# Weights stored in the order of their tiles and a weight stream of seven buffers, in a decoder block on one core

## The chip, the cores and the metric

The kernel runs on one core of one Trainium2 chip. The metric is device time in microseconds; each version is timed in several runs and one further execution is profiled.

## What is computed

One layer of a hybrid decoder block on 256 tokens of width 2048, in float32. Cut to what matters:

```
ada = silu(c) @ w_ada + b_ada                      # c: one row of 2048; w_ada: 2048 x 12288
sh1, sc1, gt1, sh2, sc2, gt2 = split(ada, 6)
u = rmsnorm(x, g_mix) * (1 + sc1) + sh1            # 256 x 2048
q, kc, vc, ks, vs, kw, vw, g_nsa, u_ssm, g_merge = split(u @ w_in)     # w_in: 2048 x 11312
kc, vc = compress(kc, w_ck1, w_ck2), compress(vc, w_cv1, w_cv2)        # w_c*1: 32 x 128 x 128
y_a = attention(q; compressed, selected, window keys and values; g_nsa)
y_s = gelu(s5_ssm(u_ssm))                          # complex diagonal recurrence, 128 groups x 64 states
y_b = y_s * sigmoid(y_s @ w_glu + b_glu)
h = x + gt1 * ((sig(gA) * y_a + sig(gB) * y_b) @ w_out)
h = h + gt2 * (relu(rmsnorm(h) * (1 + sc2) + sh2 @ w_up)^2 @ w_down)
return rmsnorm(h, g_final)
```

## The kernel before, in words

All weights go once through SBUF as a stream of **units**: one unit is a tile `raw` of 128 partitions x 1024 float32 (512 KB) with what is done to it (class `Unit`, line 199; `load` is lines 206 to 209, issued on SyncE's queue). Units of a product ("gemm" units) are split in two float32r parts: ScalarE copies `raw` to `hi` (line 116, helper `copy`), VectorE makes `lo = raw - hi` (line 119, helper `tt`), and TensorE multiplies three times, hi x hi, hi x lo, lo x hi (lines 310, 312, 313; for values lines 893 to 895). Other units are read by TensorE straight from `raw`: the first third of the conditioning (`ada1_units`, products at line 339), most of the other two thirds (`ada2_pe_units`, line 998) and the compression weights (`compress_units`, line 1101, two units at a time). A few conditioning units are accumulated on VectorE (`ada2_units`, line 128).

The order of the units is a list written out by hand at the end of `block_kernel`: conditioning woven with the first pass of the projection (S5 channels, kc/vc, the keys ks and kw, chunk by chunk of the 2048 rows), then values vs and vw woven with compression, the gate unit, the projections gA, q, gB (each woven with conditioning units), w_glu with the attention running beside it, w_out, w_up, w_down. There are 697 units; `run_units` (line 225) walks through them in this order and emits, at unit i, first the loads that are due, then hi, then the product of the unit two places back (`SPLIT`), then lo, then steps of the background generators: the S5 parameters, its scan and outputs, loads and stores of intermediate tensors, the attention. All engines take their instructions in the order in which they are emitted. Which background step stands at which unit is set by counts of units, not by time.

Three things set when a load starts. The pool `raw` has `RAW = 4` buffers, so the load of unit i + 3 is emitted at unit i and waits on SyncE until the last reader of the unit that held the buffer is done: VectorE's lo, or TensorE's product. SyncE works in order, so every later transfer on its queue waits behind that load: S5 parameters (lines 512 to 522), stores of S5 matrices (`s5_keep`, line 756), their reloads (`s5_matrices`, line 833), the attention's tensors (`attn_setup`, lines 1032 to 1045). And the transfers of SyncE and ScalarE share eight completion counters, used in turn, so a transfer also waits for the one eight places before it.

The source of a load decides the length of its rows in HBM. `four_k` reads four blocks of 128 x 256 columns of `w_ada` (rows of 1 KB), `ada2_pe_units` eight blocks of 128 x 128 (512 B), `compress_units` eight 128 x 128 matrices (512 B), the gate unit 16 x 48 columns (192 B); keys and values take two transfers of 128 x 512 (2 KB rows) each. All other weights come in rows of 4 KB, or 2 KB for `w_glu`.

The outputs of the S5 part (`s5_outputs`, line 836) run beside the gB projection, units 269 to 296: 16 steps, each of which turns a slice of the states for the next step (`turn`, two ScalarE copies into a tile `xs` of 4 KB per partition, two buffers), multiplies on TensorE (lines 858, 863, 868), adds on VectorE (line 128) and ends in a gelu on ScalarE (line 873).

Of the kernel before, what the change touches and what calls it, by code (L numbers as in the profile page):

```python
# [9 lines left out]
FT = mybir.dt.float32  # L10
# [15 lines left out]

RAW, HI, LO = 4, 3, 3
SPLIT = 2
# [52 lines left out]
@with_exitstack  # L81
def block_kernel(ctx, tc, cst_in, x, c, w_ada, b_ada, g_mix, w_in, w_ck1, w_ck2, pe_ck,
                 w_cv1, w_cv2, pe_cv, a_re, a_im, log_dt, b_re, b_im, c_re, c_im, d_skip,
                 w_glu, b_glu, w_out, g_mlp, w_up, w_down, g_final, out):
    nc = tc.nc
# [139 lines left out]
    def run_units(bgs):  # L225
        n = len(units)
        for b in bgs:
            b["done"] = 0
        ready = []
        loaded = count = 0  # L230
# [6 lines left out]
        for i, u in enumerate(units):  # L237
            now[0] = u.index = i
            while loaded < min(n, i + RAW):
                units[loaded].load()  # L240
                loaded += 1
            u.prep()
            if u.lo_first:
                u.prep_lo()
            if u.gemm:
                ready.append(u)
                while len(ready) > SPLIT or any(r.joint for r in ready[:-1]):
                    run_next()
            else:
                u.do(u)  # L250
            if not (u.lo_first):
                u.prep_lo()
            while i in later:
                for fn in later.pop(i):
                    fn()
            count += u.gemm
            for b in bgs:
                if b["start"] <= i:
                    if b.get("tick"):
                        span, at = b["end"] - b["start"] + 1, i - b["start"] + 1  # L260
                    else:
                        b.setdefault("from", count - 1)
                        span, at = max(1, gemms[min(b["end"], n - 1)] - b["from"]), count - b["from"]
                    want = min(b["total"], -(-b["total"] * at // span))
                    while b["done"] < want:
                        b["done"] += 1
                        next(b["gen"], None)
                    if i >= b["end"]:
                        for _ in b["gen"]:
                            pass  # L270
# [8 lines left out]
    def gemm_pass(src, col0, kts, ncol, k_first, k_last, xs, banks, finish, xprep=None, halves=None,  # L279
# [6 lines left out]
        def src_of(kt0):  # L286
            if halves is None:
                if per == 1:
                    return [(lambda r: r, src[kt0 * 128:(kt0 + 1) * 128, col0:col0 + ncol])]
                v = src[kt0 * 128:(kt0 + per) * 128, col0:col0 + ncol].rearrange("(k p) n -> p k n", p=128)  # L290
                return [(lambda r: r.rearrange("p (k n) -> p k n", k=per), v)]
            return [((lambda r, j=j: r[:, 512 * j:512 * j + 512]),
                     src[kt0 * 128:(kt0 + 1) * 128, h:h + 512]) for j, h in enumerate(halves)]

# [34 lines left out]

    def four_k(off, t0, n=256):  # L330

        return [(lambda r: r.rearrange("p (k n) -> p k n", k=4),
                 w_ada[0, t0 * 128:(t0 + 4) * 128, off:off + n].rearrange("(k p) n -> p k n", p=128))]

# [53 lines left out]
    def first_pass_units(ci):  # L388
        k0, k1 = chunks[ci]
        res = []  # L390
        for g in PASS:
            def finish(b, ps, g=g):
# [5 lines left out]
                else:  # L398
                    st = stage()
                    tt(st, ps, acc, OP.add)  # L400
                    A.dma_start(out=d_k[:, 2 * b:2 * b + 2, :], in_=st.rearrange("p (k t) -> p k t", k=2))
            kw = dict(halves=(C_KS, C_KW)) if g == 3 else {}
            col0 = (C_SSM, C_SSM + 1024, C_KC, 0)[g]
# [433 lines left out]
    def s5_outputs():  # L837
# [4 lines left out]
        def turn(ct):  # L842

            t = sp.tile([128, 1024], FT, tag="xs", name="xs", bufs=2).rearrange("p (r q c) -> p r q c", r=2, q=4)
            for r_ in range(2):
# [35 lines left out]
    def vs_units():  # L881
        made = {}

        def run(u, kt):
# [3 lines left out]
            for t in range(2):  # L888
                xh, xl = uh[:, kt, t * 128:t * 128 + 128], ul[:, kt, t * 128:t * 128 + 128]
                for s in range(2):  # L890
# [5 lines left out]
                    if kt == 15:  # L896
                        st = stage()
                        copy(st, o)
                        A.dma_start(out=d_v[:, t, s, :], in_=st)
        return [Unit([((lambda r, j=j: r[:, 512 * j:512 * j + 512]),  # L900
                       w_in[0, kt * 128:(kt + 1) * 128, h:h + 512]) for j, h in enumerate((C_VS, C_VW))],
                     lambda u, k=kt: run(u, k)) for kt in range(16)]

    def gate_unit():
        def run(u):
# [11 lines left out]
            def fin():  # L917
                p2 = bank("T0")
                for t in range(2):
                    PE.transpose(p2[:, 48 * t:48 * t + 48], st[0:48, t * 128:t * 128 + 128], ident[0:48, 0:48])  # L920
                ts(gates.rearrange("p i n -> p (i n)"), p2[:, 0:96], 0.5, OP.mult, 0.5, OP.add)
            defer(1, fin)
        return [Unit([(lambda r: r[:, 0:768].rearrange("p (k n) -> p k n", n=48),
                       w_in[0, :, C_GT:C_GT + 48].rearrange("(k p) n -> p k n", p=128))], run, width=768)]

# [58 lines left out]
    def ada2_pe_units(vec, quarter):  # L984
        off = (A_GT1, A_SH2, A_SC2, A_GT2)[vec] + 512 * quarter
        hold = {}
# [17 lines left out]
        def fin():  # L1004
# [7 lines left out]
            if vec == 2 and quarter == 3:  # L1012
                stt(s2, sc2_c, 1.0, gmlp_c, OP.add, OP.mult)
        return [Unit([(lambda r: r.rearrange("p (k n) -> p k n", k=8),
                       w_ada[0, 1024 * half:1024 * half + 1024, off + 128 * j:off + 128 * j + 128].rearrange(
                           "(k p) n -> p k n", p=128))], lambda u, j=j, half=half: run(u, j, half), gemm=False)
                for j in range(4) for half in range(2)]
# [66 lines left out]
    def compress_units():  # L1084
        hold = {}
        res = []
        for l0 in range(0, 32, 8):
            for s, w in enumerate((w_ck1, w_cv1)):
                def run(u, l0=l0, s=s):
# [13 lines left out]
                    if l0 == 24:  # L1103
                        fin1()
                res.append(Unit([(lambda r: r.rearrange("p (l e) -> p l e", l=8),
                                  w[0, l0:l0 + 8].rearrange("l d e -> d l e"))], run, gemm=False))

# [470 lines left out]


# [17 lines left out]
```

## Time and profile before

| | |
|---|---|
| median of 3 timed runs | 1832.56 us (1830.14 to 1833.49) |
| the profiled execution's own time | 1824.45 us |
| its span, first to last instruction | 1822.7 us |
| TensorE busy | 1731.7 us (95%) |
| VectorE, ScalarE, GpSimd busy | 1110.5, 859.0, 29.4 us |
| moved by the DMA engines | 406.27 MB, mean 223 GB/s |
| packets: all; under 2 KB | 231,755; 143,920 |

Busy times are sums over the span, and a stretch in which TensorE is busy all the time need not be one in which it is at its peak, since the ends of its pipelined products are modelled. Idle time that an instruction spends before it starts is put down to what released it last. The share of the DMA engines is a mean over the core's 16 engines; the profile counts a transfer by the packets that it is cut into, and a packet is one row of the source where that row is 4 KB or less. "To landing" is the time from the issue of a transfer to its arrival.

### The profile page before, as it was taken

What the parts mean: (1) busy time and instruction counts of PE and PEld (TensorE: products, weight loads), DVE (VectorE), ACT (ScalarE), POOL (GpSimd) and SP (SyncE); (2) the same over time, 40 slices, a digit from 0 to 9 for tenths busy, and PEclk for the clock granted to TensorE, in tenths of its full rate; (3) what the DMA queues carried; (4) which work ended last, traced back from release to release, by engine and by line L of the source; (5) the groups of instructions that cost most, each with busy time, mean ns of one, the idle gap of its engine ahead of it and who ended that gap; (6) DMA issues with size and microseconds to landing.
All of it is one profiled execution on the core that took longest, in us unless ns stands there. A gap on an engine that the chain in (4) does not pass through costs nothing.

```text
span 1822.7 us, 37716 instructions
## 1 busy us (share of the span) xinstructions
PE 1731.7 (95%) x15710; PEld 1625.9 (89%) x15710; DVE 1110.5 (61%) x2032; ACT 859.0 (47%) x1379; POOL 29.4 (2%) x51
## 2 busy tenths in 40 slices
PE   5799999799999999999999999999999999999997
PEld 3678889579999998878888999999999999999997
DVE  4758567517778886676565675554555555565554
ACT  3333443283334348655554444444444544464444
POOL 1000000120000000000000000000000000000000
PEclk8999999899999999999999989999999999999998
DMA  8888765847979787886667747777777566555663
GB/s 295 268 265 295 242 214 186 247 115 224 310 242 279 240 254 246 264 263 215 209 197 247 240 150 233 230 242 221 230 242 229 188 183 181 183 174 186 184 184 116
DMA packets 231755, 406.27 MB, mean 223 GB/s; under 512 B 16464, under 2 KB 143920, under 8 KB 230816
## 3 DMA queue, kind: packets, MB, share of 16 engines
q1 hardware_dynamic: 224432, 385.49, 67.7%
q10 hardware_dynamic: 5408, 9.75, 1.4%
q0 software_dynamic: 1744, 8.62, 1.4%
q8 instruction: 123, 2.02, 0.5%
q14 instruction: 48, 0.39, 0.1%
HBM read 384.84 MB, written 16.88 MB: 220 GB/s over the span
## 4 chain that ended last, share of the span: by engine, by line
PE 74%; DMA 11%; DVE 7%; ACT 6%; issue 1%; SPq 0%; ACTq 0%; DVEq 0%
PE A L310 22%; PE A L312 21%; PE A L313 21%; DMA raw<-in_w_ada_dram 5%; DVE lo L119 3%; DMA raw<-in_w_in_dram 3%; ACT hi L116 2%; DMA raw<-in_w_out_dram 1%; PE T L339 1%; PE T L998 1%; DMA raw<-in_w_cv_dram 1%; DVE RX L119 1%; ACT RX L116 1%; PE T L805 1%; PE A L893 1%
## 5 line engine op out<-in xcount | busy, mean ns | idle before, releaser
L119 DVE TENSOR_TENSOR lo<-raw,hi 128x1024 fp32r<-128x1024 f32 (+1 forms) x497 | 607.2, 1223 | 551.6 <-ACT hi L116 549.7
L116 ACT ACTIVATE hi<-raw 128x1024 fp32r<-128x1024 f32 (+1 forms) x497 | 524.0, 1056 | 648.6 <-PE A L312 469.4
L310 PE MATMUL A<-RU,hi 128*128 128x256 f32 x2560 | 740.8, 289 | 2.2 <-ACT RU L382 1.5
L313 PE MATMUL A<-RU,lo 128*128 128x256 f32 x2560 | 727.9, 284 | 0.8 <-DVE lo L119 0.8
L312 PE MATMUL A<-RU,hi 128*128 128x256 f32 x2560 | 728.0, 284 | 0.0
L310 PEld LDWEIGHTS A<-RU,hi 128*128 128x128 f32 x2560 | 494.9, 193 | 27.6 <-issue 21.3
L313 PEld LDWEIGHTS A<-RU,lo 128*128 128x128 f32 x2560 | 494.6, 193 | 1.1 <-DVE lo L119 1.0
L312 PEld LDWEIGHTS A<-RU,hi 128*128 128x128 f32 x2560 | 495.3, 193 | 0.3 <-DVE RU L128 0.2
L310 PE MATMUL A<-RB,hi 128*128 128x256 f32 x1280 | 363.9, 284 | 1.4 <-ACT RB L116 1.2
L312 PE MATMUL A<-RB,hi 128*128 128x256 f32 x1280 | 362.5, 283 | 0.2
L313 PE MATMUL A<-RB,lo 128*128 128x256 f32 x1280 | 362.1, 283 | 0.0
L310 PEld LDWEIGHTS A<-RB,hi 128*128 128x128 f32 x1280 | 245.6, 192 | 3.4 <-ACT RB L116 1.6
L312 PEld LDWEIGHTS A<-RB,hi 128*128 128x128 f32 x1280 | 245.6, 192 | 0.6 <-DVE RB L128 0.6
L313 PEld LDWEIGHTS A<-RB,lo 128*128 128x128 f32 x1280 | 245.6, 192 | 0.0
L116 ACT ACTIVATE RB<-RX 128x256 fp32r<-128x256 f32 x160 | 64.3, 403 | 27.4 <-DVE RX L128 27.4
L339 PE MATMUL T<-raw,cond 128*32 128x256 f32 x512 | 43.0, 418 | 27.1 <-DMA raw<-in_w_ada_dram 27.1
L119 DVE TENSOR_TENSOR RX<-A,RX 128x512 f32<-128x512 f32 x60 | 40.7, 690 | 36.1 <-PE A L313 35.2
L128 DVE SCALAR_TENSOR_TENSOR s<-raw,cond,s 128x1024 f32<-128x1024 f32 x45 | 57.6, 1279 | 0.1
L116 ACT ACTIVATE RX<-T 128x256 f32<-128x256 f32 (+2 forms) x81 | 39.8, 636 | 32.9 <-PE T L1206 23.3
L998 PE MATMUL T<-raw,cond 128*32 128x128 f32 x1280 | 45.8, 277 | 9.4 <-DMA raw<-in_w_ada_dram 7.3
L119 DVE TENSOR_TENSOR RB<-RX,RB 128x256 fp32r<-128x256 f32 x128 | 53.5, 419 | 1.6 <-ACT RB L116 1.6
L998 PEld LDWEIGHTS T<-raw,cond 128*32 128x32 f32 x1280 | 31.6, 109 | 19.2 <-DMA raw<-in_w_ada_dram 10.7
(237 smaller groups left out, 1258.4 us busy)
## 6 DMA issues: line engine op xcount, KB each, us to landing
raw<-in_w_ada_dram SPq DMA_DIRECT2D x192, 512.0 KB, 4.9
raw<-in_w_in_dram SPq DMA_DIRECT2D x144, 512.0 KB, 4.5
raw<-in_w_up_dram SPq DMA_DIRECT2D x128, 512.0 KB, 4.1
raw<-in_w_down_dram SPq DMA_DIRECT2D x128, 512.0 KB, 4.3
raw<-in_w_in_dram SPq DMA_DIRECT2D x64, 256.0 KB, 4.0
raw<-in_w_glu_dram SPq DMA_DIRECT2D x32, 512.0 KB, 5.7
raw<-in_w_out_dram SPq DMA_DIRECT2D x32, 512.0 KB, 5.0
RB<-d_c SPq DMA_DIRECT2D x8, 512.0 KB, 5.5
```

Of the source, the lines that this page charges most:

```text
L116: A.activation(out=out, in_=in_, func=AF.Copy, scale=scale)
L119: V.tensor_tensor(out=out, in0=a, in1=b, op=op)
L128: V.scalar_tensor_tensor(out=out, in0=a, scalar=s, in1=b, op0=op0, op1=op1)
L310: PE.matmul(out=o, lhsT=w.hi[:, at], rhs=xh, start=first and j % 2 == 0, stop=False, skip_group_check=True)
L312: PE.matmul(out=o, lhsT=w.hi[:, at], rhs=xl, start=False, stop=False, skip_group_check=True)
L313: PE.matmul(out=o, lhsT=w.lo[:, at], rhs=xh, start=False, stop=last, skip_group_check=True)
L339: PE.matmul(out=ps[q:q + 32, :], lhsT=cond[:, t0 + t:t0 + t + 1].to_broadcast([128, 32]), rhs=r[:, t, :], start=t0 == 0, stop=t0 == 12, ti ...
L805: PE.matmul(out=ps[h][:, (w * 2 + r_) * 128:(w * 2 + r_) * 128 + 128], lhsT=bl[c4 // 2][64 * h:64 * h + 64, (gw + w) % 16, r_, :], rhs=stk ...
L893: PE.matmul(out=o, lhsT=xh, rhs=u.hi[:, at], start=kt == 0, stop=False)
L998: PE.matmul(out=ps[q:q + 32, 0:128], lhsT=cond[:, kt:kt + 1].to_broadcast([128, 32]), rhs=r[:, kt % 8, :], start=kt < 4, stop=kt >= 12, ti ...
```

## The change

The host hands over seven rearranged arrays, built in `layouts`: `l_ada1`, `l_ada2`, `l_ck1`, `l_cv1`, `l_gate`, `l_keys`, `l_vals`. In each the 128 x 1024 values of one unit (768 for the gate) stand one after the other in HBM, partition by partition, so that a load is one transfer with rows of 4 KB (3 KB), and keys and values take one transfer instead of two. `w_ada` is still passed whole, for the units that VectorE accumulates; `w_in` for the others. No arithmetic changes.

`RAW` goes from 4 to 7. The room is that of the two `xs` tiles, which go, and 4 KB per partition from the scratch of GpSimd's transfers (8192 to 4096). The turned S5 states now take buffers of the `raw` pool; from seven units before the S5 outputs to their end the stream therefore runs four units ahead instead of six (`RAW - 2` in the place of `RAW`).

```diff
-RAW, HI, LO = 4, 3, 3
+RAW, HI, LO = 7, 3, 3
...
     def run_units(bgs):
         n = len(units)
+        outs = next(b for b in bgs if b["name"] == "outs")
+        def at_least(i):
+            return outs["start"] - RAW <= i <= outs["end"]
...
-            while loaded < min(n, i + RAW):
+            while loaded < min(n, i + (RAW - 2 if at_least(i) else RAW)):
...
-            return [((lambda r, j=j: r[:, 512 * j:512 * j + 512]),
-                     src[kt0 * 128:(kt0 + 1) * 128, h:h + 512]) for j, h in enumerate(halves)]
+            return [(lambda r: r, halves[kt0])]
...
-    def four_k(off, t0, n=256):
-        return [(lambda r: r.rearrange("p (k n) -> p k n", k=4),
-                 w_ada[0, t0 * 128:(t0 + 4) * 128, off:off + n].rearrange("(k p) n -> p k n", p=128))]
+    def four_k(off, t0):
+        return [(lambda r: r, l_ada1[off // 256, t0 // 4])]
...
-            t = sp.tile([128, 1024], FT, tag="xs", name="xs", bufs=2).rearrange(...)
+            t = raw_tile().rearrange("p (r q c) -> p r q c", r=2, q=4)
...
-        return [Unit([(lambda r: r.rearrange("p (k n) -> p k n", k=8),
-                       w_ada[0, 1024 * half:1024 * half + 1024, off + 128 * j:off + 128 * j + 128].rearrange(
-                           "(k p) n -> p k n", p=128))], lambda u, j=j, half=half: run(u, j, half), gemm=False)
+        return [Unit([(lambda r: r, l_ada2[4 * (4 * vec + quarter) + j, half])],
+                     lambda u, j=j, half=half: run(u, j, half), gemm=False)
...
-                res.append(Unit([(lambda r: r.rearrange("p (l e) -> p l e", l=8),
-                                  w[0, l0:l0 + 8].rearrange("l d e -> d l e"))], run, gemm=False))
+                res.append(Unit([(lambda r: r, w[l0 // 8])], run, gemm=False))
...
+def layouts(inputs):
+    ada, w_in = np.asarray(inputs["w_ada"])[0], np.asarray(inputs["w_in"])[0]
+    def both(c0, c1):
+        return np.concatenate([w_in[:, c:c + 512].reshape(16, 128, 512) for c in (c0, c1)], axis=2)
+    res = {
+        "l_ada1": ada[:, :4096].reshape(4, 4, 128, 16, 256).transpose(3, 0, 2, 1, 4).reshape(16, 4, 128, 1024),
+        "l_ada2": ada[:, 4096:10240].reshape(2, 8, 128, 48, 128).transpose(3, 0, 2, 1, 4).reshape(48, 2, 128, 1024),
+    }
...
-    nc = _bacc.Bacc("TRN2", target_bir_lowering=False, num_devices=1, dynamic_dma_scratch_size=8192)
+    nc = _bacc.Bacc("TRN2", target_bir_lowering=False, num_devices=1, dynamic_dma_scratch_size=4096)
```

**SyncE's queue at the start of the program.** Each row is a transfer with its destination, source, shape and, in brackets, the counters that it waits for (DMAHW: one of the eight completion counters; PE: a product that last read the buffer). Before:

```order
3 L429 DMA RS<-in_x_dram 128x2048 x2
4 L209 DMA raw<-in_w_ada_dram 128x4x256 x2
5 L209 DMA raw<-in_w_ada_dram 128x4x256 [waits DMAHW0_49]
6 L209 DMA raw<-in_w_ada_dram 128x4x256 [waits DMAHW1_49]
7 L209 DMA raw<-in_w_ada_dram 128x4x256 [waits DMAHW6_49,DMAHW2_49,PE_49]
8 L209 DMA raw<-in_w_ada_dram 128x4x256 [waits DMAHW7_49,DMAHW3_49,PE_49]
```

After:

```order
3 L433 DMA RS<-in_x_dram 128x2048 x2
4 L210 DMA raw<-in_l_ada_dram 128x1024 x2
5 L210 DMA raw<-in_l_ada_dram 128x1024 [waits DMAHW0_49]
6 L210 DMA raw<-in_l_ada_dram 128x1024 [waits DMAHW1_49]
7 L210 DMA raw<-in_l_ada_dram 128x1024 [waits DMAHW2_49]
8 L210 DMA raw<-in_l_ada_dram 128x1024 [waits DMAHW3_49]
9 L210 DMA raw<-in_l_ada_dram 128x1024 [waits DMAHW4_49]
10 L210 DMA raw<-in_l_ada_dram 128x1024 [waits DMAHW6_49,DMAHW5_49,PE_49]
```

The first load that waits for a product is the eighth instead of the fifth; the transfer of the input `x` still stands ahead of all of them.

**SyncE's queue at the values and the compression.** `in_w_in` with 128x512 is a half of a values unit, `in_w_ck` and `in_w_cv` (then `in_l_ck`, `in_l_cv`) are compression units, `d_c<-RX` is the first of the four stores of S5 matrices. Before:

```order
96 L209 DMA raw<-in_w_ck_dram 128x8x128
97 L209 DMA raw<-in_w_in_dram 128x512 x2
98 L209 DMA raw<-in_w_cv_dram 128x8x128
99 L209 DMA raw<-in_w_in_dram 128x512 x2
100 L209 DMA raw<-in_w_ck_dram 128x8x128
101 L209 DMA raw<-in_w_cv_dram 128x8x128
102 L209 DMA raw<-in_w_in_dram 128x512 x2
103 L209 DMA raw<-in_w_ck_dram 128x8x128
104 L209 DMA raw<-in_w_in_dram 128x512 x2
105 L756 DMA d_c<-RX 128x1024
```

After:

```order
98 L210 DMA raw<-in_l_cv_dram 128x1024
99 L210 DMA raw<-in_l_vals_dram 128x1024
100 L210 DMA raw<-in_l_ck_dram 128x1024
101 L210 DMA raw<-in_l_cv_dram 128x1024
102 L210 DMA raw<-in_l_vals_dram 128x1024
103 L210 DMA raw<-in_l_ck_dram 128x1024
104 L210 DMA raw<-in_l_vals_dram 128x1024
105 L210 DMA raw<-in_l_cv_dram 128x1024
106 L210 DMA raw<-in_l_vals_dram 128x1024
107 L210 DMA raw<-in_l_ck_dram 128x1024
108 L760 DMA d_c<-RX 128x1024
```

The first store of an S5 matrix, which stands at the same unit in both, now comes behind seven compression units instead of five, and behind one more values unit; each values unit is one row instead of two.

**ScalarE's queue in the S5 outputs.** The gelu (`RS<-st`), the hi part of a gemm unit and the two copies of a turned state. Before:

```order
388 L873 ACTIVATE RS<-st 128x2x128 [waits DVE_49]
389 L116 ACTIVATE hi<-raw 128x1024 [waits DMAHW7_49]
390 L116 ACTIVATE xs<-RX 128x512 [waits PE_49,Activation_49]
391 L116 ACTIVATE xs<-RX 128x512
392 L873 ACTIVATE RS<-st 128x2x128 [waits DVE_49]
```

After:

```order
394 L877 ACTIVATE RS<-st 128x2x128 [waits DVE_49]
395 L117 ACTIVATE hi<-raw 128x1024 [waits DMAHW1_49]
396 L117 ACTIVATE raw<-RX 128x512 [waits DMAHW0_49,DVE_49,Activation_49]
397 L117 ACTIVATE raw<-RX 128x512
398 L877 ACTIVATE RS<-st 128x2x128 [waits DVE_49]
```

The order is the same; the copy of a state waits for a load and for VectorE, the last users of a weight buffer, where it waited for TensorE, the last user of a state buffer.

## Rows read from the trace of the kernel before

**Rows 1.** The page: busy time of each engine with its share of the span and its instructions, and the chain of work that ended last, by engine.

```profile
PE 1731.7 (95%) x15710; PEld 1625.9 (89%) x15710; DVE 1110.5 (61%) x2032; ACT 859.0 (47%) x1379; POOL 29.4 (2%) x51
...
PE 74%; DMA 11%; DVE 7%; ACT 6%; issue 1%; SPq 0%; ACTq 0%; DVEq 0%
```

**Rows 2.** Busy time of each engine by stretch. Columns: stretch and its length (us), busy us of PE, PEld, DVE, ACT and POOL with instructions, the granted TensorE clock (1.00 is full speed), the share of the DMA engines, GB/s. Conditioning with the first pass is 0 to some 310, values with compression the rest to 360, the S5 inputs to 410, gA and q to 650, gB with the S5 outputs to 765, w_glu with the attention to 960, w_out to 1060, then w_up and w_down.

```profile
0.00:100.00 100.00, 67.10 (x584) 49.36 (x588) 58.05 (x172) 33.66 (x52) 5.79 (x9) 0.91 0.88 282
100.00:200.00 100.00, 94.07 (x940) 81.42 (x934) 69.28 (x94) 37.05 (x54) 2.95 (x4) 0.97 0.80 267
200.00:300.00 100.00, 97.64 (x1012) 89.99 (x1011) 56.26 (x86) 44.86 (x76) 2.14 (x4) 1.00 0.72 228
300.00:360.00 60.00, 47.67 (x320) 40.10 (x319) 40.36 (x51) 18.85 (x30) 8.72 (x16) 0.86 0.73 219
360.00:410.00 50.00, 46.42 (x387) 37.99 (x386) 10.14 (x12) 38.10 (x74) 9.23 (x17) 1.00 0.45 124
410.00:650.00 240.00, 232.21 (x2256) 224.56 (x2255) 190.51 (x528) 91.40 (x110) 0.00 (x0) 0.99 0.83 261
650.00:765.00 115.00, 112.00 (x1359) 101.74 (x1359) 79.64 (x136) 77.82 (x100) 0.00 (x0) 1.00 0.77 242
765.00:960.00 195.00, 186.84 (x1701) 160.22 (x1700) 125.67 (x374) 105.75 (x315) 0.56 (x1) 1.00 0.72 227
960.00:1060.00 100.00, 96.76 (x951) 92.61 (x950) 60.35 (x98) 45.40 (x73) 0.00 (x0) 0.99 0.75 231
1060.00:1800.00 740.00, 737.88 (x6109) 735.01 (x6110) 410.38 (x462) 355.81 (x481) 0.00 (x0) 0.99 0.65 202
```

**Rows 3.** TensorE's waits over the whole span: us in total, times, longest us.

```profile
PE T L339 <- DMA raw<-in_w_ada_dram: 27.1, 18, 6.2
PE T L998 <- DMA raw<-in_w_ada_dram: 7.3, 10, 1.7
...
PE T L920 <- ACT st L915: 2.8, 1, 2.8
```

**Rows 4.** Transfers by source over the whole span (the page): KB of each, median us from issue to landing.

```profile
raw<-in_w_ada_dram SPq DMA_DIRECT2D x192, 512.0 KB, 4.9
raw<-in_w_in_dram SPq DMA_DIRECT2D x144, 512.0 KB, 4.5
raw<-in_w_up_dram SPq DMA_DIRECT2D x128, 512.0 KB, 4.1
...
raw<-in_w_in_dram SPq DMA_DIRECT2D x64, 256.0 KB, 4.0
```

**Rows 5.** The columns of Rows 2 for five stretches: the input x and conditioning rows of 1 KB with a full queue; conditioning rows of 1 KB with a full queue; values and compression; the time of the stores of S5 matrices; w_up, rows of 4 KB.

```profile
5.00:10.00 5.00, 0.00 (x0) 0.00 (x0) 0.19 (x1) 2.72 (x4) 0.00 (x0) 1.00 1.00 392
80.00:85.00 5.00, 1.67 (x20) 1.17 (x23) 2.58 (x9) 0.00 (x0) 0.00 (x0) 0.77 1.06 263
302.00:336.00 34.00, 29.15 (x202) 25.11 (x201) 33.74 (x43) 9.76 (x14) 0.00 (x0) 0.90 0.52 152
335.00:340.00 5.00, 5.00 (x23) 3.83 (x22) 1.87 (x3) 4.64 (x13) 3.64 (x7) 0.98 1.06 353
1100.00:1400.00 300.00, 300.00 (x2496) 298.83 (x2495) 160.61 (x134) 139.42 (x161) 0.00 (x0) 1.00 0.74 234
```

**Rows 6.** TensorE's instructions by line, 0 to 100 us: count, busy us, mean ns, then the idle time before them and what ended it.

```profile
L339 PE MATMUL T<-raw,cond 128*32 128x256 f32 x252 | 22.4, 443 | 25.4 <-DMA raw<-in_w_ada_dram 25.4
```

**Rows 7.** The same, 300 to 360 us.

```profile
L1101 PE MATMUL T<-raw,RX 128*60 128x128 f32 x128 | 13.3, 350 | 12.3 <-DMA raw<-in_w_ck_dram 7.2 <-DMA raw<-in_w_cv_dram 5.1
```

**Rows 8.** VectorE's instructions around the compression, in order of time: start us, us, and in brackets the idle time before it.

```profile
302.22 2.35 DVE L119 TENSOR_TENSOR lo<-raw,hi 128x1024 fp32r<-128x1024 f32 x2
...
317.98 1.22 DVE L119 TENSOR_TENSOR RX<-RS,lam 128x1024 f32<-128x1024 f32 x1
...
335.37 1.22 DVE L119 TENSOR_TENSOR lo<-raw,hi 128x1024 fp32r<-128x1024 f32 x1
339.71 1.22 DVE L119 TENSOR_TENSOR lo<-raw,hi 128x1024 fp32r<-128x1024 f32 x1 [3.13 <-ACT hi L116]
346.02 1.23 DVE L119 TENSOR_TENSOR lo<-raw,hi 128x1024 fp32r<-128x1024 f32 x1 [5.09 <-ACT hi L116]
```

**Rows 9.** The chain of work that ended last, 300 to 365 us, in order of time: start us, us, what.

```profile
344.02 9.36 DMA raw<-in_w_cv_dram
353.43 3.67 PE T L1101 x30
```

**Rows 10.** ScalarE's instructions in the S5 outputs, in order of time (columns as in Rows 8).

```profile
710.83 0.45 ACT L873 ACTIVATE RS<-st 128x256 f32<-128x256 f32 x1
711.16 1.04 ACT L116 ACTIVATE hi<-raw 128x1024 fp32r<-128x1024 f32 x1
712.11 2.17 ACT L116 ACTIVATE xs<-RX 128x512 f32<-128x512 f32 x2
715.25 0.44 ACT L873 ACTIVATE RS<-st 128x256 f32<-128x256 f32 x1 [0.98 <-DVE st L128]
```

**Rows 11.** SyncE's waits before a load over the whole span: us in total, times, longest us.

```profile
SPq L209 <- DVE lo L119: 511.2, 216, 14.7
...
SPq L209 <- PE T L339: 71.6, 48, 4.3
SPq L209 <- PE T L998: 70.1, 36, 5.5
```

More of the change, by code (lines that the diff above doesn't have):

```diff
@@ L81, in block_kernel @@
 @with_exitstack
-def block_kernel(ctx, tc, cst_in, x, c, w_ada, b_ada, g_mix, w_in, w_ck1, w_ck2, pe_ck,
-                 w_cv1, w_cv2, pe_cv, a_re, a_im, log_dt, b_re, b_im, c_re, c_im, d_skip,
-                 w_glu, b_glu, w_out, g_mlp, w_up, w_down, g_final, out):
+def block_kernel(ctx, tc, cst_in, x, c, w_ada, b_ada, g_mix, w_in, w_ck2, pe_ck,
+                 w_cv2, pe_cv, a_re, a_im, log_dt, b_re, b_im, c_re, c_im, d_skip,
+                 w_glu, b_glu, w_out, g_mlp, w_up, w_down, g_final,
+                 l_ada1, l_ada2, l_ck1, l_cv1, l_gate, l_keys, l_vals, out):
     nc = tc.nc
@@ L401, in finish @@
                     A.dma_start(out=d_k[:, 2 * b:2 * b + 2, :], in_=st.rearrange("p (k t) -> p k t", k=2))
-            kw = dict(halves=(C_KS, C_KW)) if g == 3 else {}
+            kw = dict(halves=l_keys) if g == 3 else {}
             col0 = (C_SSM, C_SSM + 1024, C_KC, 0)[g]
@@ L842, in turn @@
         def turn(ct):
-            t = sp.tile([128, 1024], FT, tag="xs", name="xs", bufs=2).rearrange("p (r q c) -> p r q c", r=2, q=4)
+            t = raw_tile().rearrange("p (r q c) -> p r q c", r=2, q=4)
             for r_ in range(2):
@@ L899, in run @@
                         A.dma_start(out=d_v[:, t, s, :], in_=st)
-        return [Unit([((lambda r, j=j: r[:, 512 * j:512 * j + 512]),
-                       w_in[0, kt * 128:(kt + 1) * 128, h:h + 512]) for j, h in enumerate((C_VS, C_VW))],
-                     lambda u, k=kt: run(u, k)) for kt in range(16)]
+        return [Unit([(lambda r: r, l_vals[kt])], lambda u, k=kt: run(u, k)) for kt in range(16)]
     def gate_unit():
@@ L922, in run @@
             defer(1, fin)
-        return [Unit([(lambda r: r[:, 0:768].rearrange("p (k n) -> p k n", n=48),
-                       w_in[0, :, C_GT:C_GT + 48].rearrange("(k p) n -> p k n", p=128))], run, width=768)]
+        return [Unit([(lambda r: r[:, 0:768], l_gate)], run, width=768)]
     spare = {"n": 0}
@@ L984, in ada2_pe_units @@
     def ada2_pe_units(vec, quarter):
-        off = (A_GT1, A_SH2, A_SC2, A_GT2)[vec] + 512 * quarter
         hold = {}
@@ L1087, in compress_units @@
         for l0 in range(0, 32, 8):
-            for s, w in enumerate((w_ck1, w_cv1)):
+            for s, w in enumerate((l_ck1, l_cv1)):
                 def run(u, l0=l0, s=s):
@@ L1577 @@
         "g_mlp", "w_up", "w_down", "g_final"]
+def layouts(inputs):
[6 more added lines that the diff above has]
+    }
+    for n in ("ck1", "cv1"):
+        w = np.asarray(inputs["w_" + n])[0]
+        res["l_" + n] = w.reshape(4, 8, 128, 128).transpose(0, 2, 1, 3).reshape(4, 128, 1024)
+    res["l_gate"] = w_in[:, C_GT:C_GT + 48].reshape(16, 128, 48).transpose(1, 0, 2).reshape(128, 768)
+    res["l_keys"] = both(C_KS, C_KW)
+    res["l_vals"] = both(C_VS, C_VW)
+    return res
 def kernel(**inputs):
@@ L1584 @@
     from concourse.bass_utils import run_bass_kernel_spmd as _run
-    nc = _bacc.Bacc("TRN2", target_bir_lowering=False, num_devices=1, dynamic_dma_scratch_size=8192)
+    nc = _bacc.Bacc("TRN2", target_bir_lowering=False, num_devices=1, dynamic_dma_scratch_size=4096)
     arrays = {"in_cst_dram": constants()}
     for name in _INS:
+        if name in ("w_ck1", "w_cv1"):
+            continue
         arrays[f"in_{name}_dram"] = np.ascontiguousarray(inputs[name])
+    for name, a in layouts(inputs).items():
+        arrays[f"in_{name}_dram"] = np.ascontiguousarray(a)
     args = [nc.dram_tensor(n, a.shape, _mybir.dt.from_np(a.dtype), kind="ExternalInput").ap()
```

## The prediction

> **What bounds the kernel now.** I began with the page. TensorE is busy for 95% of the span, and the chain that ended last is 74% TensorE and 11% transfers [rows 1]. The 11% must not be read as what can be won: a transfer lies on that chain wherever a unit arrives just in time, and costs only where TensorE stands idle for it. So I went to the stretches [rows 2] and to TensorE's own waits [rows 3].
>
> The stretches show three regimes. From 1060 us on TensorE is busy for 737.9 of 740 us and the DMA engines have room (0.65): a weight stream that runs further ahead has nothing to give there. From 0 to 100 us TensorE is busy for 67 us and the DMA engines for 0.88 of the time: transfers set the pace. From 300 to 360 us TensorE is busy for 47.7 of 60 us at a granted clock of 0.86, with the DMA engines at only 0.73: something holds the transfers back. All other stretches lose a few per cent.
>
> TensorE's waits for transfers are 27.1 us for the first conditioning (line 339), 7.3 us for the later conditioning (line 998) [rows 3] and 12.3 us for the compression (line 1101) [rows 7], 46.7 us together. That is nearly all this change can reach directly.
>
> What holds loads back is on SyncE: its loads wait for the reader of the buffer four units earlier, 511 us in all for VectorE's lo and 142 us for the products of lines 339 and 998 [rows 11].
>
> **The change part by part.**
>
> *Start, 0 to 100 us.* 282 GB/s for 100 us are 28.2 MB [rows 2]. TensorE waits 25.4 us for conditioning rows [rows 6]; that is the most that can go. With seven buffers the queue need not run empty, so the share may go from 0.88 to 1. At today's rate per full share, 282/0.88 = 320 GB/s, the 28.2 MB take 88 us: 12 us saved. What rows of 4 KB are worth on top is in no single row. With a full queue, rows of 1 KB moved 263 GB/s at a share of 1.06; the best nearby stretches moved 353 (largely rows of 4 KB) and 392 (x, in long rows) [rows 5]; but w_up, in rows of 4 KB, moves 234 at 0.74, which is 316 at a full share [rows 5], no more than the 320. At 353 the bytes take 80 us, 20 us saved. The first weights still arrive behind x, and the parameters of the S5 part still pass through the same queue, so I take 13 us, near the end that w_up supports. Bounds: 5 us (half of the gaps stay) and 25.4 us.
>
> The rule that speaks against this part is in the Trainium skill, DMA: Bandwidth & Descriptors, Specifications: a transfer has the full line rate from 512 B on. By it the new order of the rows saves nothing, and only the depth counts; the 316 against 320 agrees with it, the 263 against 353 does not. By the rule this term would be 12 us instead of 13.
>
> *100 to 200 us.* The rest of the wait at line 339, 27.1 - 25.4 = 1.7 us, goes; after it TensorE, not the queue, sets the pace (share 0.80 and 0.72) [rows 2]. Bounds: 0 and 1.7 us.
>
> *Compression, 300 to 360 us.* VectorE is busy practically all of 302 to 336 us (lo parts and the S5 matrices) [rows 5], then waits 3.1 and 5.1 us for hi parts whose transfers are late [rows 8]; the last compression weights spend 9.4 us in the queue, and the last products run from 353.4 to 357.1 us [rows 9]. The compression loads start late because their buffers are released by lo's that stand in VectorE's full queue. With seven buffers three more units are in SBUF when that queue fills up, and the weights of 512 B rows and the split values rows take one transfer each with rows of 4 KB. What ends last is then VectorE: its lo of 335.37 is done at 336.6, and the two late ones take 1.2 us each, to 339. TensorE still has the products of one values unit and one pair of compression units behind that, some 4 us (the last pair took 3.7 us at the lowered clock): about 343 instead of 357.1, 14 us. The clock then falls less often; at 0.86 the 60 us lost at most 8 us, part of it while idle. I take 12 us, since the stores of S5 matrices stand further back in SyncE's queue and must be out before the states are written. Bounds: 4 us (VectorE's gaps of 3.1 and 5.1 us halved) and 18 us (12.3 us of waits and most of the clock). What is late next is VectorE's lo.
>
> *410 to 650 and 960 to 1060 us.* The waits of line 998, 7.3 us in all [rows 3]. The DMA engines have room (0.83 and 0.75) [rows 2], so a deeper stream should cover them: 6 us. Bounds: 2 and 7.3 us. The 2.8 us that line 920 waits for ScalarE stay [rows 3].
>
> *S5 outputs in 650 to 765 us.* No wait of TensorE for a transfer there, and the depth is about as before: the stream runs four units ahead instead of three, while the states take two of the seven buffers. A state's two copies now wait for the last reader of a weight buffer. ScalarE's round in this stretch is 4.42 us (one gelu at 710.83, the next at 715.25), of which gelu, hi and copies take 0.45 + 1.04 + 2.17 = 3.66 us [rows 10]. If each copy had to wait for a lo of 1.2 us [rows 8], the round would be 4.9 us, 0.45 us more, 7 us in 16 steps. That is the bound; I take 0, because the buffer that becomes free is mostly the one of a unit before.
>
> *Free.* One transfer in the place of two for keys and values (32 units) saves SyncE issues, which nobody waits for. Smaller scratch for GpSimd: it issues the transfers of the S5 inputs, and 360 to 410 us is ScalarE's stretch (38 of 50 us busy) with a DMA share of 0.45 [rows 2], which covers a slower issue; without that cover, a few us. Other transfers on SyncE's queue (S5 matrices, attention tensors) come behind up to three more loads; a load takes some 4 to 5 us to land [rows 4], mostly latency, so I bound that at 5 us once and count 0.
>
> Sum: 13 + 1.7 + 12 + 6 = 32.7 us. The profiled execution has a span of 1822.7 us and took 1824.45 us in all; it would come to 1791.8 us. The median of the timed runs stands 8.1 us above it, at 1832.56 us; there the sum gives **1800 us**, and I forecast on that scale.
>
> **The rivals.**
>
> *All stalls go.* The upper bounds: 25.4 + 1.7 + 18 + 7.3 = 52 us, 1780 us. For it: with a full queue 353 and 392 GB/s were seen [rows 5]. Against: 0 to 100 us must still move 28.2 MB.
>
> *Only the depth pays*, by the rule above of the Trainium skill. As a mechanism: a transfer's time is set by bytes, rows of 512 B and 1 KB cost the same as rows of 4 KB. Then the start gives 12 us at best and nearer to 9 with gaps left, the compression, whose loads still take longer to land, 9, the rest 6: 24 us, 1808 us. For it: conditioning lands in 4.9 us, w_up in 4.1 [rows 4], a small difference.
>
> *The depth does not take effect.* A load needs a free buffer, a free completion counter of the eight and SyncE's turn; and loads wait mostly for lo [rows 11], whose place on VectorE does not move. If the stream stays about as far ahead as before, only the rows pay: at the start 100 x (1 - 320/353) = 9 us, less what is hidden, and little at the compression: 4 us or less, 1829 us, which a measurement can hardly tell from no change.
>
> *Slower.* In the S5 outputs the loads now also wait for TensorE's products with the turned states, since those hold buffers of the stream. TensorE runs two gemm units behind, so such a load could be emitted in time and released late. If the 16 loads that follow a state each exposed a whole landing of 4.5 us [rows 4], that would be 72 us in this stretch; less the 32.7 us, 1832.6 + 39 = 1872 us. It decides from the point where a load is released less than 4.5 us before ScalarE's hi needs it. Against it: TensorE has two units, some 8.8 us by ScalarE's round [rows 10], between such a product and the unit in question, and four units stand in between in the stream.
>
> **How the numbers follow.** The forecast, 1800 us: 0.50. All stalls, 1780 us: 0.13. Only the depth, 1808 us: 0.22. No effect, 1829 us: 0.08. Slower, 1872 us: 0.07. Its own range from the bounds: the low ends sum to 5 + 0 + 4 + 2 - 7 - 5 = -1 us, the high ends to 52 us, but not all ends come together; leaving out the slower case and most of the no-effect case gives 1780 to 1820 us. About 0.2% (3.7 us) is what a measurement of this kernel can tell from no change. Faster by more than that: 0.50 + 0.13 + 0.22 and half of the no-effect case, 0.89; within it 0.04; slower 0.07.
>
> **What would show it.** Right: TensorE's wait at line 1101's place nearly gone, and VectorE without its gaps of 3.1 and 5.1 us; TensorE's wait for first conditioning about halved, the DMA share of the first 80 us near 1; packets under 2 KB down from 143,920 to well under half; the stretch from w_up on as long as before. Wrong: the wait at line 339 still 20 us or more (then the rate, not the gaps, holds the start); VectorE's lo or ScalarE's hi in the place of the transfers among TensorE's waits; new waits in the S5 outputs; any gain after 1060 us, which I have no reason for.

## The result, and the profile after

| | before | after |
|---|---|---|
| median of the timed runs | 1831.35 us (4 runs) | 1777.62 us (4 runs, 1776.92 to 1780.11) |
| ratio | | 0.9735, interval 0.9702 to 0.9767 |
| the profiled execution's own time | 1824.45 us | 1776.92 us |
| its span | 1822.7 us | 1775.1 us |
| TensorE busy; not busy | 1731.7; 91.0 us | 1718.9; 56.2 us |
| its waits for weight transfers | 46.7 us | 10.0 us |

The kernel is faster by 2.65% (2.3 to 3.0%). The ratio is the one on record; the quotient of the two medians would be 0.9707, but the two later comparisons of the same change below gave 0.9727 and 0.9734. 1800 us were forecast, and 1777.62 us is below the low end of the range, 1780 us. The forecast stood on 1832.56 us for the kernel before: as ratios it was 0.982 with a range of 0.971 to 0.993, and 0.9735 lies inside it, near the end of the larger gain. On the scale of the profiled executions, on which the sum was made, 47.6 us of span went where 32.7 us were forecast.

The page of the kernel after, as in [rows 1], with the line on the packets between:

```profile
PE 1718.9 (97%) x15710; PEld 1620.6 (91%) x15710; DVE 1108.5 (62%) x2032; ACT 856.3 (48%) x1379; POOL 29.4 (2%) x51
...
DMA packets 121802, 406.26 MB, mean 229 GB/s; under 512 B 13904, under 2 KB 18480, under 8 KB 120864
...
PE 87%; DVE 5%; ACT 4%; DMA 2%; issue 1%; ACTq 0%; SPq 0%; DVEq 0%
```

Transfers fell from 11% of the chain to 2%. TensorE's 15,710 products are the same in number, yet their busy time fell by 12.8 us: that is no waiting, it is how long the same products were counted as busy. The other 34.8 us are idle time.

TensorE's waits after, as in [rows 3] (L343 is before's line 339, L998 still 998, and line 1101 is now L1100):

```profile
PE T L343 <- DMA raw<-in_l_ada_dram: 10.0, 3, 6.3
...
PE T L922 <- ACT st L917: 2.5, 1, 2.5
...
PE A L899 <- DVE lo L120: 2.3, 2, 1.6
PE T L867 <- ACT raw L117: 2.1, 3, 1.1
```

One line for weight transfers is left, three waits at the start. The compression and the later conditioning have none. The values products (L899) now wait 2.3 us for VectorE's lo.

Busy time by stretch, after, columns and stages as in [rows 2]; the boundaries are moved with the work, so the lengths compare:

```profile
0.00:85.00 85.00, 65.14 (x567) 49.83 (x568) 57.01 (x172) 33.38 (x47) 5.79 (x9) 0.92 0.93 337
85.00:185.00 100.00, 96.83 (x998) 84.44 (x998) 70.72 (x98) 40.14 (x65) 2.95 (x4) 1.00 0.86 296
280.00:325.00 45.00, 42.05 (x323) 35.18 (x322) 39.00 (x49) 17.93 (x30) 5.68 (x11) 1.00 0.66 211
...
1013.00:1752.00 739.00, 736.61 (x6104) 733.74 (x6105) 410.19 (x463) 355.87 (x482) 0.00 (x0) 1.00 0.64 200
```

The start moves 337 GB/s where it moved 282; the compression takes 45 us at a clock of 1.00 where it took 60 at 0.86; w_up and w_down take 739 us where they took 740.

Transfers after, as in [rows 4]. Conditioning lands in 4.9 us as before (48 of before's 192 are the units for VectorE, which were not rearranged), and w_in, whose rows did not change, in 4.6 where it took 4.5.

```profile
raw<-in_l_ada_dram SPq DMA_DIRECT2D x144, 512.0 KB, 4.9
raw<-in_w_in_dram SPq DMA_DIRECT2D x144, 512.0 KB, 4.6
```

VectorE around the compression, columns as in [rows 8]:

```profile
315.18 1.22 DVE L120 TENSOR_TENSOR lo<-raw,hi 128x1024 fp32r<-128x1024 f32 x1
319.07 1.23 DVE L120 TENSOR_TENSOR lo<-raw,hi 128x1024 fp32r<-128x1024 f32 x1 [2.67 <-ACT hi L117]
321.37 1.23 DVE L120 TENSOR_TENSOR lo<-raw,hi 128x1024 fp32r<-128x1024 f32 x1 [1.07 <-ACT hi L117]
```

TensorE's products of the compression by line, as in [rows 7], 280 to 340 us:

```profile
L1100 PE MATMUL T<-raw,RX 128*60 128x128 f32 x128 | 7.9, 276 | 0.0
```

VectorE is still packed until 315 us (busy for 34.69 of the 35 us from 280 us on), but TensorE no longer waits a single time for a compression weight, and its 128 products take 7.9 us where they took 13.3 [rows 7].

**Where in the program the time was won.** Both kernels' TensorE runs the same products in the same order. So I took the end of the k-th product in both traces; the difference is the lead over before at that point, which I worked out from the traces (us). "Busy less" is by how much less of the stage TensorE counts as busy; the rest of a gain is idle time:

| at, in before | what ends there | lead after | gain in the stage | of it busy less | forecast |
|---|---|---|---|---|---|
| 101 us | first conditioning | 14.5 | 14.5 | 1.4 | 13 |
| 193 us | conditioning with pass 1 | 20.1 | 5.6 | 2.9 | 1.7 |
| 314 us | rest of pass 1, before the compression | 20.2 | 0.1 | 0.0 | 0 |
| 361 us | compression | 36.1 | 15.9 | 6.7 | 12 |
| 406 us | S5 inputs | 36.0 | -0.1 | -0.3 | 0 |
| 596 us | gA, q | 43.4 | 7.4 | 2.5 | 6, with the stage to 1048 us |
| 773 us | S5 outputs | 44.3 | 0.9 | 0.4 | 0 |
| 815 us | a part of the attention | 42.8 | -1.5 | -2.6 | 0 |
| 1048 us | attention, w_out | 46.6 | 3.8 | 1.3 | in the 6 |
| end | w_up, w_down | 47.5 | 0.9 | 0.5 | 0 |

**The clock.** TensorE's granted clock is at one of its two levels, 1.2 or 2.4 GHz, a row with a value between has both. Three stretches of the kernel before, and then the stretches in which the one after does the same products:

```profile
185.00:195.00 10.00, 8.01 (x58) 6.82 (x59) 4.58 (x10) 6.14 (x12) 0.00 (x0) 0.83 0.66 213
325.00:335.00 10.00, 5.98 (x38) 4.75 (x37) 9.93 (x9) 2.89 (x5) 0.00 (x0) 0.67 0.52 149
345.00:360.00 15.00, 8.90 (x49) 6.98 (x48) 2.89 (x4) 3.88 (x5) 2.65 (x5) 0.66 1.03 308
```

```profile
167.50:174.90 7.40, 6.49 (x58) 5.30 (x59) 3.67 (x8) 4.94 (x10) 0.00 (x0) 1.00 0.71 255
303.60:307.60 4.00, 3.32 (x38) 2.46 (x37) 3.97 (x4) 1.06 (x1) 0.00 (x0) 1.00 0.90 335
317.60:323.20 5.60, 5.60 (x49) 4.48 (x48) 2.92 (x4) 4.12 (x9) 3.80 (x8) 1.00 0.93 322
```

Leaving out the last products of the program, the time at the lower level fell from 58.0 to 30.7 us. Half of those 27.3 us would be 13.7 us, near the 12.8, but that is not their price: TensorE is busy in only 43.9 of the 58.0 us and in 28.2 of the 30.7. Compared product by product in the two traces, the lower level accounts for some 7.4 us of the 12.8: products that ran at it in before alone got 14.1 us shorter, those that ran at it in after alone 6.7 us longer. The other 5.4 us are products at the higher level in both kernels, nearly all of lines 339, 998 and 1101, whose waits went. Line 998 before, then after:

```profile
L998 PE MATMUL T<-raw,cond 128*32 128x128 f32 x1280 | 45.8, 277 | 9.4 <-DMA raw<-in_w_ada_dram 7.3 <-ACT RX L116 2.0
```

```profile
L998 PE MATMUL T<-raw,cond 128*32 128x128 f32 x1280 | 43.2, 276 | 2.0 <-ACT RX L117 2.0
```

One such product takes 277 ns, but 1280 of them are busy for 45.8 us, 36 ns each, because they overlap. The first one behind a wait overlaps nothing and counts whole; 13 such products make up 2.5 of the 2.6 us. In the two other profiles of the change TensorE's busy time is 13.0 and 10.4 us less than in the one profile of before, 9.1 and 6.0 us of it by the clock.

### The profile page after: what moved, and what is told of

Read it like the earlier page. It is cut to its first block, busy times and chain, and to the rows that moved or that the text cites. A ratio compares the mean times of both kernels' runs of the same rounds, so it can differ in the third digit from the quotient of the medians.

```text
span 1775.1 us, 37647 instructions
## 1 busy us (share of the span) xinstructions
PE 1718.9 (97%) x15710; PEld 1620.6 (91%) x15710; DVE 1108.5 (62%) x2032; ACT 856.3 (48%) x1379; POOL 29.4 (2%) x51
## 4 chain that ended last, share of the span: by engine, by line
PE 87%; DVE 5%; ACT 4%; DMA 2%; issue 1%; ACTq 0%; SPq 0%; DVEq 0%
PE A L315 25%; PE A L317 24%; PE A L318 24%; PE T L998 2%; DVE lo L120 2%; PE T L343 2%; ACT hi L117 1%; ACT RX L117 1%; DMA raw<-in_l_ada_dram 1%; PE T L809 1%; PE A L897 1%; DMA raw<-in_l_vals_dram 1%; PE A L899 1%; PE A L898 1%; PE T L737 0%
## 5 line engine op out<-in xcount | busy, mean ns | idle before, releaser
L343 PE MATMUL T<-raw,cond 128*32 128x256 f32 x512 | 40.8, 413 | 10.0 <-DMA raw<-in_l_ada_dram 10.0
L998 PE MATMUL T<-raw,cond 128*32 128x128 f32 x1280 | 43.2, 276 | 2.0 <-ACT RX L117 2.0
L998 PEld LDWEIGHTS T<-raw,cond 128*32 128x32 f32 x1280 | 32.5, 109 | 8.4 <-ACT RX L117 4.2
```

Source lines behind the costliest of these rows:

```text
L343: PE.matmul(out=ps[q:q + 32, :], lhsT=cond[:, t0 + t:t0 + t + 1].to_broadcast([128, 32]), rhs=r[:, t, :], start=t0 == 0, stop=t0 == 12, ti ...
L998: PE.matmul(out=ps[q:q + 32, 0:128], lhsT=cond[:, kt:kt + 1].to_broadcast([128, 32]), rhs=r[:, kt % 8, :], start=kt < 4, stop=kt >= 12, ti ...
```

## The experiments

In all of them the kernel computes the whole reference. "Lead" is the lead over before, as in the table above.

**The new order of the rows alone.**

```
-RAW, HI, LO = 7, 3, 3
+RAW, HI, LO = 4, 3, 3
...
-while loaded < min(n, i + (RAW - 2 if at_least(i) else RAW)):
+while loaded < min(n, i + RAW):
...
-t = raw_tile()...
+t = sp.tile([128, 1024], FT, tag="xs", name="xs", bufs=2)...
...
-dynamic_dma_scratch_size=4096
+dynamic_dma_scratch_size=8192
```

> Only the new order of the rows: seven arrays in tile order, but four buffers and the states in tiles of their own, as before. Theory 'depth' (most of the 48 us come from loads that start earlier): some 10 to 15 us under the kernel before, a ratio of 0.992 to 0.995, with TensorE still waiting about 8 us or more for compression weights, since those loads are held back by VectorE's lo. Theory 'rows' (a transfer of 512 B or 1 KB rows takes longer, and that was the bound): 30 us or more, a ratio of 0.984 or less, the lead at the start of the program nearly all of the changed kernel's 15 us.

Measured: 1810.67 us, ratio 0.9899 (0.988 to 0.9918). TensorE's waits:

```profile
PE T L343 <- DMA raw<-in_l_ada_dram: 24.5, 14, 6.7
PE T L1100 <- DMA raw<-in_l_ck_dram: 6.0, 2, 4.4
...
PE T L1100 <- DMA raw<-in_l_cv_dram: 3.6, 4, 1.1
...
PE T L998 <- DMA raw<-in_l_ada_dram: 3.4, 7, 0.9
```

The order of the rows is worth 1.0% with four buffers, and the wait of the start stays: 24.5 of 27.1 us.

**The depth alone**, rows of before.

```
-RAW, HI, LO = 4, 3, 3
+RAW, HI, LO = 7, 3, 3
+at_least(i), RAW - 2 there, raw_tile() for the states, scratch 4096   (as in the change)
```

> Only the depth: seven buffers, two lent to the states, all weights in their old rows. Theory 'depth': 24 to 35 us under the kernel before, a ratio of 0.981 to 0.987, and the compression stage as short as in the changed kernel. Theory 'rows': 15 us or less, a ratio of 0.992 or more, with TensorE's wait for the first conditioning still near 25 us and a DMA share near 1 in the first 100 us. If the two gains add up, this one and the rows-only one sum to the 48 us; if each removes what the other would, the sum is more.

Measured: 1779.88 us, ratio 0.9725 (0.9701 to 0.9749), the change's own within the intervals. Of the waits for weight transfers one line is left:

```profile
PE T L344 <- DMA raw<-in_w_ada_dram: 11.4, 4, 6.7
```

The depth alone does all that the change does. The order alone takes 1.0% and the depth alone 2.75%, together they take 2.65%: they remove the same waits. The windows of this kernel at the start, then of the one after, then of the order alone:

```profile
0.00:85.00 85.00, 64.75 (x556) 49.01 (x557) 57.16 (x172) 33.39 (x47) 5.79 (x9) 0.90 1.00 336
10.00:25.00 15.00, 10.51 (x88) 6.25 (x88) 8.37 (x15) 3.76 (x5) 3.51 (x1) 1.00 1.10 356
40.00:55.00 15.00, 15.00 (x136) 13.74 (x135) 12.42 (x40) 10.52 (x17) 0.00 (x0) 1.00 1.04 362
```

```profile
10.00:25.00 15.00, 10.96 (x97) 6.75 (x101) 8.77 (x17) 3.90 (x6) 3.51 (x1) 0.98 1.03 411
...
40.00:55.00 15.00, 15.00 (x136) 13.74 (x134) 12.38 (x41) 10.59 (x17) 0.00 (x0) 1.00 0.89 332
```

```profile
0.00:85.00 85.00, 59.82 (x492) 44.54 (x493) 49.63 (x152) 31.67 (x46) 5.80 (x9) 0.87 0.86 294
```

Rows of 4 KB can be faster (411 against 356 GB/s from 10 to 25 us; 413 against 355 when both were run again, below), but over the first 85 us both orders move about the same, 336 and 337 GB/s (327 and 342 again); with 4 KB rows the DMA engines are only less busy for it (0.93 against 1.00).

**Depth alone and the change again, side by side**, to see a difference of a few us.

```
depth alone: as above        the change: unaltered
```

> Seven buffers with the rows of before, once more, on the same chip as the changed kernel. Theory (depth carries nearly everything, the order of the rows a little): ratio to before 0.973 to 0.976, 0 to 5 us behind the changed kernel on this chip, first-conditioning wait 11 to 12 us. Rival (the order of the rows pays beside the depth what it pays alone, 18 us): 18 us behind, ratio 0.983. Rival (it costs something): ahead of the changed kernel, ratio under 0.971.

> The changed kernel, unaltered, on the same chip as the one with seven buffers and the rows of before. All theories: ratio 0.970 to 0.975, 1775 to 1781 us.

Measured: 1779.77 us, ratio 0.974 (0.9719 to 0.9762), for the depth alone; 1779.9 us, ratio 0.9734 (0.971 to 0.9757), for the change. Beside seven buffers the order of the rows buys nothing that these runs can tell from zero; the intervals leave room for some 5 us either way.

**How many buffers?** Five, and none lent:

```
-RAW, HI, LO = 7, 3, 3
+RAW, HI, LO = 5, 3, 3
 (states in tag "xs", i + RAW as in the order alone; scratch stays 4096)
```

> New rows, five buffers, the states in tiles of their own (nothing lent; the 4 KB from the GpSimd scratch give the fifth buffer). If the stream's reach is what counts up to seven units, this stands about half way between rows alone and the changed kernel. If one more buffer is enough to cover a landing, it is within 5 us of the changed kernel, and the lending is worth little.

Measured: 1788.11 us, ratio 0.9779 (0.9754 to 0.9804).

```profile
PE T L343 <- DMA raw<-in_l_ada_dram: 13.9, 9, 6.2
PE T L1100 <- DMA raw<-in_l_cv_dram: 4.6, 2, 3.7
...
PE T L1100 <- DMA raw<-in_l_ck_dram: 2.1, 2, 1.1
```

Six, with two lent and the old scratch:

```
-RAW, HI, LO = 7, 3, 3
+RAW, HI, LO = 6, 3, 3
-dynamic_dma_scratch_size=4096
+dynamic_dma_scratch_size=8192
```

> New rows, six buffers with two lent to the states (four in the S5 outputs), the GpSimd scratch back at 8192. If the depth pays step by step, TensorE's lead over the kernel before after the compression lies between that of five buffers (25 us) and of seven (36 us), and the ratio between 0.973 and 0.978. If six is enough, it is that of the changed kernel. If the smaller scratch costs anything, the S5 inputs (360 to 410 us of the old time) gain a microsecond or more here.

Measured: 1780.58 us, ratio 0.9739 (0.9712 to 0.9766). With the new rows the lead at 101 us is 3.5, 12.4, 10.0 and 14.5 us for four, five, six and seven buffers, and the gain at the compression 4.9, 7.8, 15.1 and 15.9 us. At the start the fifth buffer does most (six stand 2.4 us behind five there, about as much as two profiles of the change differ, 12.4 and 14.5 us); at the compression it is the sixth. The S5 inputs gain 0.0 us with the larger scratch (a lead of 30.5 us before and behind them), and lose 0.1 us with the smaller in the change's first profile. That does not show that the scratch is free: of nine profiles with the smaller scratch three lose 2.3 to 2.8 us there (the depth alone in its first profile, the change run again beside it, and the kernel with the first loads ahead of x, below), each with 3.4 us at the lower clock from 339 us on, and in two of these ScalarE waits some 4 us for a transfer that GpSimd issues (`d_kc<-RX`, 4.2 and 3.7 us). The other six lose 0 to 0.5 us. Whether the scratch is behind it no run settles.

**Are the compression's loads long or late?** The change with the compression weights in their old rows of 512 B:

```
-for s, w in enumerate((l_ck1, l_cv1)):
+for s, w in enumerate((w_ck1, w_cv1)):
-res.append(Unit([(lambda r: r, w[l0 // 8])], run, gemm=False))
+res.append(Unit([(lambda r: r.rearrange("p (l e) -> p l e", l=8),
+                  w[0, l0:l0 + 8].rearrange("l d e -> d l e"))], run, gemm=False))
```

> The changed kernel with the eight compression units back in rows of 512 B. Theory 'depth' (these loads were late, not long): within 3 us of the changed kernel. Theory 'rows': most of the 16 us that TensorE gained between 300 and 360 us of the old time go, a ratio to the kernel before of 0.980 or more, with waits of TensorE for in_w_ck or in_w_cv of 5 us or more.

Measured: 1776.86 us, ratio 0.9715 (0.9693 to 0.9736). TensorE's products of the compression, by line, 270 to 340 us:

```profile
L1100 PE MATMUL T<-raw,RX 128*60 128x128 f32 x128 | 7.9, 275 | 0.0
```

No wait, with rows of 512 B. They were late, not long.

**Do the stages add?** Seven buffers for the first 110 units, the start and most of pass 1, four behind them:

```
+DEEP = 110
...
 def raw_tile(k=None):   # three of the seven, tag "rawb", later hold the states
+    if k is None or (k < DEEP and k % 7 >= 4):
+        return wp.tile([128, 1024], FT, tag="rawb", name="raw", bufs=3)
+    return wp.tile([128, 1024], FT, tag="raw", name="raw", bufs=4)
...
-while loaded < min(n, i + (RAW - 2 if at_least(i) else RAW)):
+while loaded < min(n, i + (RAW if loaded < DEEP else 4)):
```

> New rows, seven buffers for units 0 to 109 and four from unit 110 on (three others lent to the states alone). If what each stage gains is its own, the start keeps its 20 us up to 300 us and the later stages gain only what rows alone gave them, some 9 us: 29 us under the kernel before, a ratio near 0.984. If the early lead is eaten by later waits, the ratio is nearer to the 0.990 of rows alone; if the lead at the start also carries the compression, it is nearer to 0.975.

Measured: 1792.4 us, ratio 0.9804 (0.9775 to 0.9833).

```profile
PE T L346 <- DMA raw<-in_l_ada_dram: 10.2, 3, 7.2
PE T L1103 <- DMA raw<-in_l_ck_dram: 5.3, 2, 3.7
...
PE T L1001 <- DMA raw<-in_l_ada_dram: 3.9, 6, 1.2
PE T L1103 <- DMA raw<-in_l_cv_dram: 3.3, 4, 1.2
```

The start keeps its gain (lead of 17.1 us before the compression), the compression falls back nearly to the gain of four buffers (5.7 us against 4.9), and the lead at the end is 29.6 us. The stages add; none gives back what another won.

**The last 10 us.** The three first conditioning loads ahead of and between the two halves of x, beside the change unaltered:

```
-loaded = count = 0
+loaded, count = 3, 0
 (in the loop over the two halves of x, ahead of its load)
+for k in ((0,), (1, 2))[t]:
+    units[k].load()
```

> The changed kernel with the first conditioning load ahead of the input x, and the second and third between its two halves. Theory 'the start is no longer bound by the rate of the transfers' (DMA share 0.93 in the changed kernel's first 85 us): TensorE's first wait for weights falls from 6.3 us to about 1, and 2 to 3 us of lead stay at 100 us and at the end. Theory 'still bound by the rate': TensorE starts earlier and waits longer later, and nothing is left at 100 us. Against the changed kernel 0.1 to 0.15% less, or the same.

> The changed kernel once more, beside the one with the first loads ahead of x, on the same chip: 0.971 to 0.975 of the kernel before.

Measured: 1776.83 us, ratio 0.9715 (0.9691 to 0.9739), against 1778.79 us, ratio 0.9727 (0.9703 to 0.975), for the change. The wait of the start fell from 10.5 to 4.1 us:

```profile
PE T L343 <- DMA raw<-in_l_ada_dram: 4.1, 3, 2.0
```

The lead at 101 us was 15.4 us against 12.4 for the change beside it (14.5 in its first profile), but at the end 47.1 against 47.7. Nothing that a timed run can tell: 6 us of waiting for weights went, 2.0 us of waiting for x came (line 452), and no time came of it. In the two profiles it was still 2.4 us ahead after the compression and lost 2.3 us in the S5 inputs, where the change beside it lost 0.1. The change run again beside the depth alone lost 2.8 us there without this edit, so that loss need not be the edit's; and profiles of the same kernel differ by 2 us at 101 us.

## Why the prediction was right in kind and too small

- *What bounds.* Right. The waits for transfers were what the change could reach, and 36.7 of 46.7 us of them went. Nothing was won after 1060 us but 0.9 us, where w_up begins: the lower clock stands there for 10.2 us before and 6.8 us after.
- *The step that was too small: idle time alone was counted.* The sum was made of waits, and the clock stood in it once, in the compression, as "at most 8 us". TensorE's busy time fell by 12.8 us in all, some 7.4 us of it by the clock and 5.4 us because fewer products had to start behind a wait. The sum lacked 14.9 us: 1.5 at the start, 3.9 from 100 to 200 us, 3.9 in the compression, 5.2 in the later conditioning, the rest elsewhere. From 100 to 200 us a wait of 1.7 us was to go and 5.6 us were won: 2.9 us are shorter products, most of them by the clock (the stretch at 185 us, clock 0.83, became one at 1.00), and line 733's wait for ScalarE there fell from 2.0 to 0.9 us.
- *Start: 13 forecast, 14.5 measured.* The size was right, its reason half wrong. It is the queue that no longer runs empty, and not the rows: with rows of 1 KB the same 336 GB/s. The 263 GB/s at a share of 1.06 [rows 5], read as what rows of 1 KB move with a full queue, was a stretch of 5 us (183 GB/s in its first half, 343 in its second) and no rate of theirs: with seven buffers they moved 356 GB/s at 1.10 from 10 to 25 us, where 4835 of 4970 packets are under 2 KB. The 320 GB/s worked out from the mean rate and its share was nearer to the 336 at 1.00.
- *Compression: 12 forecast, 15.9 measured.* Right in what it said to look for: no wait at line 1101's place, the products end some 36 us earlier, and VectorE's lo is late next (2.3 us for L899). VectorE's gaps of 3.1 and 5.1 us did not go but shrank to 2.7 and 1.1 us. The part given to rows of 4 KB was wrong (512 B rows do it as well). What the products gain beside the waits was taken too low: the clock went from 0.86 to 1.00, and TensorE is busy for 6.7 us less in this stage.
- *Later conditioning: 6 forecast, some 11 measured* (7.4 and 3.8 us). Its waits of 7.3 us went whole. The rest is TensorE's busy time, 3.8 us less in the two stages: 1.3 us by the clock, 2.5 us at the higher level in both kernels, which is what line 998's products lost in starts behind a wait.
- *Counted at nothing:* S5 outputs (0.9 us won, and their wait for the states' copies, L867, is 2.1 us where it was 2.0) and keys and values in one transfer came to nothing; GpSimd's scratch is open, as said above, and the "few us" without cover stand on no row.
- *Attention, -1.5 us.* Not foreseen, and not in every profile of the change: TensorE pauses there in both kernels, and in the first profile of the change the clock fell behind it for 6.8 us, in the two others not. The rows are before, the change first, and the change again:

```profile
780.00:785.00 5.00, 3.28 (x21) 2.39 (x19) 4.26 (x14) 2.33 (x6) 0.00 (x0) 1.00 0.78 252
```

```profile
737.00:742.00 5.00, 3.10 (x15) 2.20 (x14) 4.29 (x13) 2.64 (x6) 0.00 (x0) 0.92 0.76 229
```

```profile
737.00:742.00 5.00, 3.11 (x18) 2.15 (x16) 4.31 (x13) 2.64 (x6) 0.00 (x0) 1.00 0.78 260
```

- *The rivals.* "All stalls go", 1780 us, came nearest, and by luck in part: 10 us of stalls stayed, and shorter products, which it counted in the compression alone, made up for them. "Only the depth pays" was right in its mechanism and priced at 24 us instead of some 48. Its rule, from the Trainium skill, DMA: Bandwidth & Descriptors, Specifications, that a transfer of 512 B or more has the full line rate, agrees with these runs as far as time goes: rows of 512 B and 1 KB cost no time once the queue was kept full. From 10 to 25 us the rate itself differs from it, 356 GB/s in rows of 1 KB against 411 in rows of 4 KB, and there the measurement decides. "The depth does not take effect" and "slower" fell: SyncE still waits long for lo, as in [rows 11], but that costs nothing when it runs six units ahead.

```profile
SPq L210 <- DVE lo L120: 530.7, 217, 14.2
...
SPq L210 <- PE T L343: 89.0, 41, 4.6
SPq L210 <- PE T L998: 78.1, 40, 6.0
```

- *Open.* That the waits cause the lowered clock is shown only by their going together; no run filled TensorE's pauses with other work. The lower level also differs between profiles of one kernel (30.7, 30.7 and 37.5 us for the change), and of before there is one profile. Eight or more buffers were not tried. What holds the last 10 us at the start is not settled.

## What to carry to other kernels

Where loads are late, look first at how far the stream runs ahead and at who frees its buffers; a second copy of the weights in another order is worth trying only if the queue is full and still late. Here the depth alone took 2.6 to 2.75%, the order alone 1.0%, and both together no more than the depth. When costing TensorE's waits, add what stands behind each of them, products at the lowered clock and a first product that overlaps nothing: here that was another 12.8 us (10.4 to 13.0 in three profiles) on 34.8 us of idle time, and it is counted from the products, not as half of the time at the lower clock.

## What the runs showed of the hardware

- The stream of the first 85 us, in loads of 512 KB, moved 336 GB/s with conditioning in rows of 1 KB and seven buffers; with conditioning in rows of 4 KB it moved 294 GB/s with four buffers and 337 with seven. A busy share over 1 says nothing of the rate: 1.06 stood beside 263 GB/s before, 1.10 beside 356 with seven buffers.
- The share of the DMA engines and their rate are two things: rows of 4 KB moved the same bytes in the same time with a share of 0.93 in place of 1.00, and that room bought nothing.
- TensorE's busy time of one program differs by some us between kernels that issue the same products (1731.7 us with four buffers, 1729.9 with the order alone, 1717.3 to 1723.0 with five buffers or more throughout). The 5.7 us among the last are more than the 3.8 us by which their medians differ, the kernel of five buffers left out.
